# FFN up: low parts of the summed weight tiles made by an accumulating DMA in place of a VectorE subtraction

## The chip, the cores and the metric

The kernel runs on one core of a Trainium2 chip. The metric is the device time of one execution in microseconds. The time before is the median of three runs. All views come from one profiled execution; their times count from the start of its span.

## The reference, cut to what matters

The model is one block of a decoder trunk over 512 tokens of width 1024: a mixer with three branches, then a ConvGLU feed-forward network with 2816 inner columns. The change lies in the feed-forward part, in its first product, `h @ w_up`:

```python
def conv_glu_ffn(h, w_up, conv_w, w_down):
    a, g = jnp.split(h @ w_up, 2, axis=-1)
    return (jax.nn.silu(causal_dwconv(a, conv_w)) * g) @ w_down

x = x + g2 * conv_glu_ffn(h, ffn_w_up[l], ffn_conv_w[l], ffn_w_down[l])
```

Everything is float32, `w_up` is 1024 x 5632.

## The kernel before, in words

**Split operands.** TensorE works on the type fp32r. Each fp32 operand is split into a high part (ScalarE copies it into an fp32r tile, which rounds it) and a low part (the operand minus the high part). A product is three matmuls per k-tile: high by high, high by low, low by high.

**The FFN-up stage.** There are 22 column tiles m of 128 inner columns. The first two are computed plainly. For m = 2 to 21 the four blocks of one tile, two halves of the columns of `a` and `g` by two halves of the tokens, are computed with seven products in place of eight (a Strassen-Winograd scheme). Each product (`product`, L1049) has 4 k-tiles of three matmuls with 256 moving columns, so one m has 7 x 12 = 84 matmuls. Two of the operands on the weight side are raw blocks (w1, w2, tile `wa`), one is a raw block held in a free piece of another tile (w4, `up_22`, L1041), and four are sums of blocks:

- `up_s(m)` (L1028) loads the raw tile of `g` columns (SP queue, 512 KB) and builds two sum tiles `s12` and `s34` of 128 x 1024 fp32 (tag `fS`, two buffers, so each tile has one buffer that is used again for the next m). Four GpSimd instructions of 128 x 512 write them: L1034 and L1035 make `s12`, L1036 and L1037 make `s34`.
- `pair` (L1011) then splits a sum tile into `shi` (ScalarE, L1016) and `slo` (VectorE, L1017). These tiles lie in a ring `ws` of three buffers, so the next `shi` of a place waits until TensorE has finished the products that read the old one.
- `up_a(m)` (L1023) loads the raw tile of `a` columns and splits it with the same `pair`, into tiles `whi`, `wlo` (also L1016 and L1017).

The raw tiles share a ring of four buffers (`wraw`, L147). The loads of the `a` and `g` columns alternate on SP's queue; a load of `g` columns takes over the buffer of an earlier `a` tile and waits for L1037 (the last sum that reads that tile); a load of `a` columns takes over that of an earlier `g` tile and waits for the subtraction of `up_22` (L1046).

**The loop over m** (L1165 and after) has on TensorE, in this order: product 5 of m, product 1 of m+2, product 4 of m-1, product 6, product 3, product 2 of m+2, product 7. VectorE and ScalarE take partial results out of the banks between them: L1176 (ScalarE copies p5), L1185 (VectorE, p6), L1186 (GpSimd adds p1 to p5), L1194, L1195 and L1201 (VectorE, sums that end a block), the convolution `conv3` (L689 on ScalarE, L690 and L691 on VectorE), the silu (L1197) and the product with the gate (L1202). Product 7 writes over the bank that L1185 reads, product 4 over the bank that L1195 reads.

**What sets the order.** Every engine runs its queue in program order, and SP's and GpSimd's DMA issues stand in such queues too. The framework puts the instructions of each engine into an order by priorities: those under `tc.high_priority(offset=4000)` (sums and splits) come ahead of ordinary ones, those under `urgent()` (offset 9000: work on the banks) ahead of both. It also sets the semaphores for data dependencies and for buffers that are used again.

Of the kernel before, what the change touches and what calls it, by code (L numbers as in the profile page):

```python
# [15 lines left out]
AF = mybir.ActivationFunctionType  # L16
ALU = mybir.AluOpType
# [42 lines left out]
def hybrid_block(ctx, tc, ins, out, consts, dbg=None, stop=99):  # L60
    nc = tc.nc
    PE, ACT, DVE, POOL, SP = nc.tensor, nc.scalar, nc.vector, nc.gpsimd, nc.sync
# [17 lines left out]
    def T(name, shape, dt=F32, tag=None, bufs=1, pool=None):  # L80
        return (pool or sb).tile(shape, dt, name=name, tag=tag or name, bufs=bufs)
# [375 lines left out]
    for p in range(4):  # L457
# [52 lines left out]
        for w0 in range(0, 9, 4):  # L510
# [7 lines left out]
            lo = 1 if w0 == 0 else 0  # L518
# [61 lines left out]
    for rnd in range(2):  # L580
        for u0 in (0, 16):
# [11 lines left out]
            for hh in range(2):  # L593
                q = slice(hh * 64 + 32 * (1 - rnd), hh * 64 + 32 * (1 - rnd) + 32)
                src = ps[q].rearrange("p (u s) -> p u s", u=16)
# [412 lines left out]
    cut = lambda w, r: tuple(x[:, r] for x in w)  # L1008
    ws = ("s", 3)

    def pair(shape, src, ring=None):  # L1011

        pool, tag, bufs = (wp.pool, "w", 3) if ring is None else (fs.pool,) + ring
        with tc.high_priority(offset=4000):
            hi, lo = (T(tag + n, shape, F32R, bufs=bufs, pool=pool) for n in ("hi", "lo"))
            ACT.activation(hi, src, AF.Copy)  # L1016
            DVE.tensor_tensor(lo, src, hi, op=ALU.subtract)  # L1017
        return hi, lo

    up, raw_a, raw_22 = {}, {}, {}  # L1020
# [2 lines left out]
    def up_a(m):  # L1023
        raw_a[m] = up_raw(m * 128)
        wa = pair([128, 8, 128], raw_a[m])
        up[m] = {1: cut(wa, k1), 2: cut(wa, k2)}

    def up_s(m):  # L1028
        ra, rg = raw_a.pop(m), up_raw(DFF + m * 128)
        raw_22[m] = rg[:, 4:8]  # L1030
        a11, a12, a21, a22 = ra[:, 0:4], ra[:, 4:8], rg[:, 0:4], rg[:, 4:8]
        s12, s34 = (T("fS", [128, 8, 128], bufs=2, pool=fs.pool) for _ in range(2))
        with tc.high_priority(offset=4000):
            POOL.tensor_tensor(s12[:, 0:4], a21, a22, op=ALU.add)  # L1034
            POOL.tensor_tensor(s12[:, 4:8], s12[:, 0:4], a11, op=ALU.subtract)  # L1035
            POOL.tensor_tensor(s34[:, 0:4], a11, a21, op=ALU.subtract)  # L1036
            POOL.tensor_tensor(s34[:, 4:8], a12, s12[:, 4:8], op=ALU.subtract)  # L1037
        w12, w34 = pair([128, 8, 128], s12, ws), pair([128, 8, 128], s34, ws)
        up[m].update({5: cut(w12, k1), 6: cut(w12, k2), 7: cut(w34, k1), 3: cut(w34, k2)})

    def up_22(m):  # L1041
# [45 lines left out]
    def w_o(k0, hf, ring=None):  # L1087
        raw = load_raw([128, 2, 512], [((lambda r: r), dram("w_o", k0 * 128 * D + hf * 512, [[D, 128], [128 * D, 2], [1, 512]]))])
        return pair([128, 2, 512], raw, ring)
# [46 lines left out]
    for m in range(plain, plain + ahead):  # L1136
        up_a(m)
        if m == plain:
            up_s(m)
        x_first(m)  # L1140
        x_second(m)
# [23 lines left out]
    for m in range(plain, 22):  # L1165
        if m + ahead < 22:
            up_a(m + ahead)
        if m + 1 < 22:
            up_s(m + 1)
# [144 lines left out]
```

## Time and profile before

| what | value |
|---|---|
| median of 3 runs | 1208.91 us (1205.43 to 1214.12) |
| the profiled execution's own time | 1200.61 us |
| its span, first to last instruction | 1198.9 us |
| TensorE, share of the span busy | 90% |
| VectorE, share of the span busy | 69% |
| FFN-up loop in steady course | about 842 to 1055 us |

The span is 1.7 us shorter than the execution's own time. Busy shares are means over stages with different limits, so the stage that is changed has to be read by itself.

### The profile page before, as it was taken

To read this page: it belongs to the slowest core of one execution; us is meant where nothing else is said; L and a number is where in the kernel's file an instruction comes from. 1 tells how busy PE (TensorE), PEld (TensorE's weight loads), DVE (VectorE), ACT (ScalarE), POOL (GpSimd) and SP (SyncE) were. 2 spreads that over 40 slices of the span, in tenths; PEclk is the share of its full clock that TensorE was granted. 3 is DMA by queue.
4 is the path that set the end of the run, shared out by engine and by line. 5 is a ranking of instruction groups with operands and counts; after the bars stand their busy time and mean duration, and the time that the engine had idled before them with its cause. 6 is when DMAs were issued, how large, how long until landed. Compare 5 with 4: busy or idle time off the path is not lost. (4 is left out here: it accounts for less than half of the span.)

```text
span 1198.9 us, 18180 instructions
## 1 busy us (share of the span) xinstructions
PE 1074.5 (90%) x6962; PEld 876.1 (73%) x6962; DVE 824.0 (69%) x1405; ACT 463.2 (39%) x800; POOL 412.6 (34%) x289
## 2 busy tenths in 40 slices
PE   4888899799999989985898999998988888799996
PEld 3766677577667867873666678888987888788885
DVE  5888767732688739896465644489898999882326
ACT  4343422142334333321333433356554544552213
POOL 4233224322222433664444100024666666500001
PEclk9799999899999989997897999999999999999999
DMA  9642123421337981489654353522233323463201
GB/s 324 182 106 58 41 58 93 101 51 54 115 98 207 312 221 53 132 219 245 174 156 114 101 143 104 176 102 64 83 88 89 89 88 89 124 219 100 99 5 71
DMA packets 191078, 148.31 MB, mean 124 GB/s; under 512 B 18148, under 2 KB 167038, under 8 KB 190990
## 3 DMA queue, kind: packets, MB, share of 16 engines
q1 hardware_dynamic: 162605, 122.57, 35.3%
q10 hardware_dynamic: 23056, 14.53, 4.0%
q0 software_dynamic: 5328, 10.03, 3.6%
q8 instruction: 55, 0.90, 0.3%
q14 instruction: 34, 0.27, 0.1%
HBM read 128.48 MB, written 18.63 MB: 123 GB/s over the span
## 5 line engine op out<-in xcount | busy, mean ns | idle before, releaser
L165 POOL TENSOR_TENSOR wlo<-wraw,whi 128x1024 fp32r<-128x1024 f32 (+1 forms) x70 | 158.0, 2259 | 269.8 <-ACT whi L163 221.3
L177 PE MATMUL mm<-h_hi,whi 128*128 128x512 f32 (+2 forms) x496 | 200.9, 406 | 0.7 <-DVE o_cv L702 0.7
L178 PE MATMUL mm<-h_lo,whi 128*128 128x512 f32 (+2 forms) x496 | 200.2, 404 | 1.2 <-DVE h_lo L1082 1.2
L179 PE MATMUL mm<-h_hi,wlo 128*128 128x512 f32 (+2 forms) x496 | 199.6, 403 | 0.0
L163 ACT ACTIVATE whi<-wraw 128x1024 fp32r<-128x1024 f32 (+1 forms) x86 | 80.0, 934 | 211.4 <-PE mm L178 101.8
L178 PEld LDWEIGHTS mm<-h_lo,whi 128*128 128x128 f32 (+1 forms) x496 | 94.8, 191 | 23.2 <-issue 2.4
L177 PEld LDWEIGHTS mm<-h_hi,whi 128*128 128x128 f32 (+1 forms) x496 | 94.6, 191 | 22.4 <-issue 3.4
L179 PEld LDWEIGHTS mm<-h_hi,wlo 128*128 128x128 f32 (+1 forms) x496 | 94.8, 191 | 21.2 <-issue 1.4
L1017 DVE TENSOR_TENSOR wlo<-wraw,whi 128x1024 fp32r<-128x1024 f32 x39 | 50.8, 1302 | 42.2 <-ACT whi L1016 42.2
L217 DVE SCALAR_TENSOR_TENSOR acc<-xraw,ccol,acc 128x512 f32<-128x512 f32 x56 | 60.4, 1078 | 25.5 <-DMA xraw<-in_ada_w 25.0
L1053 PE MATMUL sd<-mg_hi,shi 128*128 128x256 f32 x240 | 69.3, 289 | 9.1 <-DVE p L1185 8.8
L1034 POOL TENSOR_TENSOR fS<-wraw 128x512 f32<-128x512 f32 x20 | 29.4, 1469 | 129.8 <-DVE wk L991 84.4
L1055 PE MATMUL sd<-mg_hi,slo 128*128 128x256 f32 x240 | 67.8, 283 | 0.0
L1054 PE MATMUL sd<-mg_lo,shi 128*128 128x256 f32 x240 | 67.8, 282 | 0.0
L1016 ACT ACTIVATE whi<-wraw 128x1024 fp32r<-128x1024 f32 x39 | 41.3, 1058 | 64.8 <-PE sd L1240 24.8
L1017 DVE TENSOR_TENSOR slo<-fS,shi 128x1024 fp32r<-128x1024 f32 x40 | 60.6, 1516 | 0.4 <-ACT shi L1016 0.3
L1053 PEld LDWEIGHTS sd<-mg_hi,shi 128*128 128x128 f32 x240 | 45.8, 191 | 11.4 <-DVE p L1185 11.3
L1053 PE MATMUL mm<-h_hi,whi 128*128 128x256 f32 x160 | 45.5, 285 | 3.4 <-ACT p L1066 3.0
L1281 POOL TENSOR_TENSOR f<-f 128x512 f32<-128x512 f32 x4 | 5.7, 1416 | 124.6 <-ACT wk L993 124.6
L721 DVE TENSOR_SCALAR mk<-posq,thr 128x512 f16<-128x512 f32 (+3 forms) x128 | 45.7, 430 | 3.1 <-PE sd L727 3.1
L1016 ACT ACTIVATE shi<-fS 128x1024 fp32r<-128x1024 f32 x40 | 42.1, 1052 | 12.6 <-PE sd L1054 12.6
L1054 PEld LDWEIGHTS sd<-mg_lo,shi 128*128 128x128 f32 x240 | 45.8, 191 | 0.0
(513 smaller groups left out, 2883.7 us busy)
## 6 DMA issues: line engine op xcount, KB each, us to landing
wraw<-in_w_in SPq DMA_DIRECT2D x61, 512.0 KB, 4.2
xraw<-in_ada_w SPq DMA_DIRECT2D x96, 256.0 KB, 4.3
wraw<-in_ffn_w_up SPq DMA_DIRECT2D x44, 512.0 KB, 3.9
wraw<-in_ffn_w_down SPq DMA_DIRECT2D x22, 512.0 KB, 3.5
wraw<-in_w_branch SPq DMA_DIRECT2D x24, 256.0 KB, 3.8
bias_d<-stage ACTq DMA_DIRECT2D x10, 512.0 KB, 5.3
wraw<-in_w_o SPq DMA_DIRECT2D x8, 512.0 KB, 3.9
z_att<-wk ACTq DMA_DIRECT2D x12, 256.0 KB, 2.4
```

The costliest lines, as they stand in the source:

```text
L163: ACT.activation(hi, raw, AF.Copy)
L165: lo_engine[0].tensor_tensor(lo, raw, hi, op=ALU.subtract)
L177: PE.matmul(ps, hi[:, k, :], ahi[:, k0 + k, :], start=start and k == 0, stop=False)
L178: PE.matmul(ps, hi[:, k, :], alo[:, k0 + k, :], start=False, stop=False)
L179: PE.matmul(ps, lo[:, k, :], ahi[:, k0 + k, :], start=False, stop=stop and k == kt - 1)
L217: DVE.scalar_tensor_tensor(acc, raw, ck, acc, op0=ALU.mult, op1=ALU.add)
L721: DVE.tensor_scalar(m_[:, :n], posq[:, b * 128:], thr[:, b, gg:gg + 1], None, op0=ALU.is_ge)
L1016: ACT.activation(hi, src, AF.Copy)
L1017: DVE.tensor_tensor(lo, src, hi, op=ALU.subtract)
L1053: PE.matmul(ps, at(w[0], k), b[0][:, k], start=first and k == 0, stop=False, skip_group_check=True)
L1054: PE.matmul(ps, at(w[0], k), b[1][:, k], start=False, stop=False, skip_group_check=True)
L1055: PE.matmul(ps, at(w[1], k), b[0][:, k], start=False, stop=k == 3, skip_group_check=True)
```

## The change

`pair` gets a flag `by_dma`. With it, ScalarE writes the negated high part into the low tile (a copy with scale -1), and GpSimd issues a DMA that adds the fp32 sum tile onto it: lo = -hi + src. The two calls in `up_s` set the flag; the splits of raw tiles, of `w_o`, `w_down` and of `up_22` stay as they are.

```diff
-    def pair(shape, src, ring=None):
+    def pair(shape, src, ring=None, by_dma=False):
 
         pool, tag, bufs = (wp.pool, "w", 3) if ring is None else (fs.pool,) + ring
         with tc.high_priority(offset=4000):
             hi, lo = (T(tag + n, shape, F32R, bufs=bufs, pool=pool) for n in ("hi", "lo"))
             ACT.activation(hi, src, AF.Copy)
-            DVE.tensor_tensor(lo, src, hi, op=ALU.subtract)
+            if by_dma:
+                ACT.activation(lo, hi, AF.Copy, scale=-1.0)
+                POOL.dma_start(lo, src, accum_op=ALU.add)
+            else:
+                DVE.tensor_tensor(lo, src, hi, op=ALU.subtract)
         return hi, lo
...
-        w12, w34 = pair([128, 8, 128], s12, ws), pair([128, 8, 128], s34, ws)
+        w12, w34 = pair([128, 8, 128], s12, ws, True), pair([128, 8, 128], s34, ws, True)
```

## Rows read from the trace of the kernel before

**Rows 1.** The page, part 1: busy time of an engine, share, instructions.

```profile
span 1198.9 us, 18180 instructions
...
PE 1074.5 (90%) x6962; PEld 876.1 (73%) x6962; DVE 824.0 (69%) x1405; ACT 463.2 (39%) x800; POOL 412.6 (34%) x289
```

**Rows 2.** By stretch: length, PE, PEld, DVE, ACT, POOL busy, clock, DMA share, GB/s.

```profile
865.00:925.00 60.00, 51.87 (x422) 49.82 (x420) 53.60 (x54) 28.39 (x45) 37.97 (x26) 1.00 0.31 89
925.00:975.00 50.00, 43.16 (x354) 41.93 (x355) 45.30 (x48) 23.48 (x37) 31.27 (x22) 1.00 0.31 91
```

**Rows 3.** Who waited for whom, 842 to 1055 us: total us, times, longest.

```profile
POOL fS L1036 <- DVE slo L1017: 28.9, 17, 4.7
...
PE sd L1053 <- DVE wk L1195: 19.3, 18, 3.1
```

**Rows 4.** Groups by line and form, 842 to 1055 us: busy, mean ns, idle before.

```profile
L1017 DVE TENSOR_TENSOR slo<-fS,shi 128x1024 fp32r<-128x1024 f32 x36 | 55.2, 1534 | 0.4 <-ACT shi L1016 0.3
```

**Rows 5.** Timeline of GpSimd: start us, us, instruction, idle before and its releaser.

```profile
839.77 1.55 POOL L1034 TENSOR_TENSOR fS<-wraw 128x512 f32<-128x512 f32 x1 [2.63 <-DMA wraw<-in_ffn_w_up]
...
957.74 1.34 POOL L1034 TENSOR_TENSOR fS<-wraw 128x512 f32<-128x512 f32 x1 [0.37 <-DMA wraw<-in_ffn_w_up]
...
963.19 1.77 POOL L1037 TENSOR_TENSOR fS<-wraw,fS 128x512 f32<-128x512 f32 x1
...
968.93 1.30 POOL L1034 TENSOR_TENSOR fS<-wraw 128x512 f32<-128x512 f32 x1 [1.36 <-DMA wraw<-in_ffn_w_up]
...
1027.61 1.30 POOL L1034 TENSOR_TENSOR fS<-wraw 128x512 f32<-128x512 f32 x1 [1.33 <-DMA wraw<-in_ffn_w_up]
```

**Rows 6.** Timeline of TensorE, first and last of 35 matmuls without a wait.

```profile
949.68 0.28 PE L1054 MATMUL sd<-mg_lo,shi 128*128 128x256 f32 x1
...
953.69 0.27 PE L1055 MATMUL mm<-h_hi,wlo 128*128 128x256 f32 x1
```

**Rows 7.** Tile fS, its instructions over the whole span: duration ns min/median/max.

```profile
L1016 ACT ACTIVATE shi<-fS x40: 1037/1047/1072, 803.1 to 1054.7; 128x1024 fp32r<-128x1024 f32 x40
L1017 DVE TENSOR_TENSOR slo<-fS,shi x40: 1207/1226/1981, 804.8 to 1055.8; 128x1024 fp32r<-128x1024 f32 x40
L1034 POOL TENSOR_TENSOR fS<-wraw x20: 1291/1392/1845, 780.2 to 1038.3; 128x512 f32<-128x512 f32 x20
L1036 POOL TENSOR_TENSOR fS<-wraw x20: 1288/1296/1402, 781.9 to 1045.6; 128x512 f32<-128x512 f32 x20
L1035 POOL TENSOR_TENSOR fS<-fS,wraw x20: 1291/1616/2162, 783.2 to 1039.7; 128x512 f32<-128x512 f32 x20
L1037 POOL TENSOR_TENSOR fS<-wraw,fS x20: 1287/1758/2272, 785.0 to 1046.9; 128x512 f32<-128x512 f32 x20
```

**Rows 8.** Line L978, plain 512 KB loads issued by GpSimd: issue ns, landing us.

```profile
L978 POOL DMA_DIRECT2D x<-in_x x4: 531/531/588, 684.0 to 693.9; - x4
...
DMA to landing us min/median/max: 3.9/4.4/6.0
```

**Rows 9.** Tile qi, eight DMAs of 192 KB issued by GpSimd into fp32r.

```profile
DMA to landing us min/median/max: 7.2/10.4/11.9
```

**Rows 10.** DMA queues in 683 to 699 us: packets, MB, share of 16 engines.

```profile
q0 software_dynamic: 580, 2.11, 41.2%
```

**Rows 11.** DMA in 842 to 1055 us: SP's queue, its issues with median landing.

```profile
q1 hardware_dynamic: 34283, 20.44, 32.2%
...
wraw<-in_ffn_w_up SPq DMA_DIRECT2D x32, 512.0 KB, 3.9
```

**Rows 12.** Line L147 on SP's queue, 842 to 1055 us: what its loads waited for.

```profile
SPq L147 <- POOL fS L1037: 89.1, 18, 11.0
```

**Rows 13.** Busy time by stretch where TensorE had gaps: columns as in rows 2.

```profile
542.00:544.00 2.00, 0.76 (x3) 0.48 (x3) 1.97 (x5) 0.12 (x1) 0.00 (x0) 1.00 1.42 200
544.00:546.00 2.00, 0.73 (x3) 0.59 (x3) 1.03 (x2) 0.00 (x0) 0.00 (x0) 0.82 1.22 290
546.00:548.00 2.00, 2.00 (x6) 1.12 (x6) 0.00 (x0) 0.00 (x0) 0.00 (x0) 0.50 1.20 300
```

## The prediction

> **What bounds the kernel now.** I read the page first. By its first part TensorE looks like the limit and VectorE is busy in two thirds of the span [rows 1]; that is a mean over stages, so the stage of the change has to be cut out. The table by stretch does that: in two stretches of the FFN-up loop VectorE is busy 53.60 of 60 us and 45.30 of 50 us (89% and 91%), TensorE 86%, with the clock at its upper level, 1.00 (2.4 GHz) [rows 2]. So here VectorE is close to full, and TensorE has gaps. The waits say who makes them: the first matmul of a product waits 19.3 us for L1195 on VectorE, in 18 iterations [rows 3]. The group that the change removes holds 55.2 us of VectorE in this stretch, 36 subtractions of 1.53 us [rows 4]; the other four of the 40 [rows 7] lie ahead of it.
>
> The period of one m: L1034 starts at 839.77 and, 16 iterations later, at 1027.61 (15 further starts between them) [rows 5], so (1027.61 - 839.77) / 16 = 11.74 us. TensorE alone would need less: 34 matmuls start between 949.68 and 953.69 [rows 6], 0.118 us each, times 84 = 9.9 us. VectorE's work is 0.9 x 11.74 = 10.6 us, of it 2 x 1.53 = 3.1 us for the two subtractions.
>
> So there are 1.8 us per m to win, if nothing else closes the loop first. Two other loops are nearly as long already. One is the sum buffers: each sum tile has one buffer, and L1036 waits 28.9 us in 17 iterations for the subtraction that reads the old `s34` [rows 3]. The other is the raw tiles: SP's load waits for L1037 (89.1 us in 18 cases) [rows 12], lands 3.9 us after issue [rows 11], and only then L1034 of the next m starts: L1037 ends at 963.19 + 1.77 = 964.96, L1034 starts at 968.93 [rows 5].
>
> **The change part by part.**
>
> *Removed:* 40 subtractions on VectorE. VectorE falls from 10.6 to 7.6 us per m and is no longer near the period. Its cover for this claim is TensorE's 9.9 us; what is late next is not VectorE. GpSimd's sums overlap fewer two-operand instructions and come nearer to their fastest: L1034 and L1035 have medians of 1.39 and 1.62 us, L1036 and L1037 1.30 and 1.76 us, all with a minimum of 1.29 us [rows 7]. I take 2.8 us for a pair of sums, between 2.6 and 3.1.
>
> *Added on ScalarE:* 40 copies of the form of `shi`, 1.05 us each [rows 7], 2.1 us per m. ScalarE is at 47% (28.39 of 60) [rows 2], 5.6 us per m; with 7.7 us it stays below TensorE's 9.9. As throughput it costs nothing; as latency it costs all of its 1.05 us, because the DMA waits for it.
>
> *Added on GpSimd:* 40 DMA issues, 0.53 us each by the plain load of the same size [rows 8]. GpSimd had 37.97 us busy in 60 [rows 2], 7.4 us per m; shorter sums and two issues leave it at about 7.5. But the issue waits for ScalarE, and behind it in the queue stand the sums of the next m and L1186, whose result L1195 needs before TensorE may go on. That is the new wait.
>
> *Added on the DMA engines:* 2 x 512 KB per m. The trace of before has no accumulating DMA and no copy inside SBUF, so D, the time from issue to landing, is bounded by neighbours. Below: a plain 512 KB load by the same queue, alone, 3.9 us at its fastest [rows 8]; nothing excludes that an SBUF source is a little quicker, but TensorE and the raw loop then bind, so a smaller D gains nothing. Above: the DMAs into fp32r in a crowd, 10.4 us in the median [rows 9]. My value: the median plain load, 4.4 us [rows 8]; plus one more pass, because the old destination is read too: 2.11 MB (four of these loads and a small one) held 41.2% of 16 us [rows 10], 6.6 us, so about 1.6 us each; plus 1.0 us, my allowance for meeting the raw loads, which hold 32.2% of the engines already [rows 11]. D = 4.4 + 1.6 + 1.0 = 7.0 us, an estimate.
>
> The Trainium skill has a statement on the second read: in "Collectives: The Full Stack", section "The bandwidth ceiling: the fold count and why AG ≠ RS ≠ AR", the addition in the DMA path is said to cost nothing by itself, but to need two source reads on one ring, so that it runs at half the rate. No run here shows it yet; the pass of 1.6 us agrees with it in kind, and by half a rate alone D would be 6.0 and the sum about 18 us smaller.
>
> *The new loop.* A sum buffer is free for the next m only when the DMA that reads it has landed. Around the loop: two sums 2.8, high part 1.05, negated copy 1.05, DMA D, and five hand-overs between engines, 0.4 in all (an allowance) = 5.3 + D. Both tiles have such a loop. To it I add 0.6 us for the two in-order queues (the copy behind other work on ScalarE, the issue behind a sum on GpSimd), my estimate from instructions of 0.4 to 1.4 us on queues that are 60 to 70% full. T = 5.3 + 0.6 + 7.0 = 12.9 us against 11.74: +1.16 us per m, times 18 iterations (m = 4 to 21, the first two are prepared under earlier work) = +21 us. The end and the other stages don't change.
>
> On the profiled execution: 1200.6 + 21 = 1221.6 us. That execution was quicker than the median of the three runs, 1208.9 us; the forecast is for a median, so 1208.9 + 21 = **1230 us**.
>
> The bounds of D give the range. With D = 3.9 the loop is 9.2 us, below TensorE's 9.9; then the raw loop binds: 3.97 us from L1037's end to L1034's start, four sums 5.3 us, two issues 1.06 us = 10.3 us, -1.4 x 18 = -26 us, 1183 us. With D = 10.4 it is 16.3 us, +4.6 x 18 = +82 us, 1291 us.
>
> **The rivals.**
>
> *Rival 1, the accumulate is quick and VectorE's relief counts (faster).* If the second read is hidden behind the write and the queue is not crowded, D is 3.9 to 4.7, the buffer loop 9.2 to 10.6 us, and the period 10.3 to 10.6: -20 to -26 us, about 1186 us. For it: the DMA engines were idle two thirds of the time [rows 11], and VectorE's 19.3 us of TensorE waits do go away [rows 3]. Against it: the fastest landing is that of an idle moment, and here two loads and two accumulates share each period. It decides at 5.3 + 0.6 + D = 11.74, so at D = 5.8.
>
> The Trainium skill speaks for this one: "DMA: Bandwidth & Descriptors", section "Anatomy of one DMA — SWDGE (gpsimd) path", gives about 2 us plus the bytes at 436 GB/s, which for two reads of 512 KB would be 2.0 + 2.4 = 4.4 us, an estimate from that page; the sum by it would be -24 us. The plain loads here landed in 4.4 us with one read, where that formula gives 3.2, so the trace is slower than the page.
>
> *Rival 2, one loop replaces another of the same length (no change).* D between 5.2 and 6.4: period 11.1 to 12.3, within 12 us of 1209. For it: two loops, that over VectorE and that over the sum buffers, were within a microsecond of each other before.
>
> *Rival 3, the two DMAs come to stand in a row (much slower).* The issue for `s34` of m may be queued on GpSimd behind L1034 and L1035 of the next m, which wait for the landing of the DMA for `s12`; then L1036 waits for a second whole landing. The loop becomes 2 D plus four sums 5.3 and an issue 0.5: 15 us at D = 4.5, 20 us at D = 7: +55 to +145 us, 1265 us and more. TensorE would then idle a third to a half of each period, and the trace shows what can follow gaps: with TensorE busy 0.76 and 0.73 of 2 us, the granted clock went from 1.00 to 0.82 and then 0.50, the lower level, 1.2 GHz [rows 13]; this would add more. Against it: by the priorities all of these have one rank, and a queue order that holds back a ready issue is not what they ask for.
>
> That the low part would not come from the DMA at all (the change not doing what it says) I hold for unlikely, since no subtraction is left to make it.
>
> **How the numbers follow.** Forecast 0.43 (its own range 1215 to 1255), rival 1 0.22, rival 2 0.2, rival 3 0.15. Within 1% is what a measurement of this kernel can hardly tell from no change; 1% is 12 us. Faster by more: 0.22, all of rival 1. Same: rival 2, 0.2. Slower: the forecast and rival 3, 0.58. The range goes from the lower to the upper bound of D, 1183 to 1291; it leaves out most of rival 3 and a little at the lower end.
>
> **What would show it.** Right: no subtraction of `fS` on VectorE and VectorE near 60% in the loop; L1034 and L1036 waiting for a DMA into `slo` in nearly every iteration; landing times of these DMAs between 6 and 8 us; the period from one L1034 to the next at 12 to 13.5 us; TensorE waiting for `slo`, no more for L1195. Wrong: landings under 5 us with a period near 10.4 us and TensorE waiting for nothing long (rival 1); a period that stands at 11.7 (rival 2); an issue that waits behind L1035 for another DMA's landing, and a period over 15 us with a clock below 1.00 (rival 3).

## The result, and the profile after

The changed kernel takes 1337.48 us in the median of four runs (1326.12 to 1343.41), the kernel before 1207.17 us beside it; the ratio is 1.1107, 95% interval 1.1045 to 1.117. That is 130 us slower. The forecast was 1230 us with a range up to 1291, so the direction was right and the size far off: the time lies where rival 3 put it. In some executions the granted clock is lower and the time one or two per cent longer; the ratios in this document leave those out on both sides, the medians do not.

The page of the kernel after, total and part 1, against [rows 1]:

```profile
span 1341.6 us, 18270 instructions
...
PE 1121.9 (84%) x6962; PEld 918.8 (68%) x6962; DVE 746.6 (56%) x1365; ACT 503.5 (38%) x840; POOL 425.8 (32%) x329
```

VectorE has 40 instructions and 77 us less, ScalarE 40 copies and 40 us more, GpSimd 40 issues. TensorE is busy 47 us longer with the same 6962 matmuls, and its granted clock is lower (0.80 and 0.77 in the rows below, 1.00 before). No engine got more than 40 us of new work, so most of the 130 us must be waiting. Busy time by stretch in the loop, columns as in [rows 2]:

```profile
920.00:980.00 60.00, 37.30 (x260) 36.02 (x259) 18.02 (x30) 23.11 (x33) 24.63 (x22) 0.80 0.47 106
980.00:1040.00 60.00, 37.91 (x257) 37.09 (x256) 17.61 (x25) 23.20 (x33) 25.04 (x23) 0.77 0.46 105
```

VectorE fell from 89% to 30%, TensorE from 86% to 62%, and the DMA engines are at less than half: nobody is full. Now the waits from 860 to 1190 us, which stand where [rows 3] stood:

```profile
PEld sd L1059 <- DMA slo<-fS: 119.0, 21, 9.0
PE sd L1059 <- DMA slo<-fS: 114.6, 20, 8.8
POOL fS L1038 <- DMA slo<-fS: 113.3, 16, 8.7
...
POOL fS L1040 <- DMA slo<-fS: 54.3, 14, 5.4
```

(L1038 to L1041 are the four sums L1034 to L1037 of before, L1059 is the matmul that reads the low part.) TensorE hardly waits for VectorE any more but for the new DMA, and so does GpSimd, twice per m: L1038 for one landing and L1040 for the other. The timeline of GpSimd over one period shows how the two stand to each other, and the first and last of 13 starts of L1038 give the period, as [rows 5] did:

```profile
893.26 1.27 POOL L1038 TENSOR_TENSOR fS<-wraw 128x512 f32<-128x512 f32 x1 [6.34 <-DMA slo<-fS]
...
990.86 1.27 POOL L1038 TENSOR_TENSOR fS<-wraw 128x512 f32<-128x512 f32 x1 [7.30 <-DMA slo<-fS]
992.21 1.28 POOL L1039 TENSOR_TENSOR fS<-fS,wraw 128x512 f32<-128x512 f32 x1
993.43 0.87 POOL L1019 DMA_DIRECT2D slo<-fS  x1
998.03 1.70 POOL L1040 TENSOR_TENSOR fS<-wraw 128x512 f32<-128x512 f32 x1 [3.73 <-DMA slo<-fS]
999.69 1.74 POOL L1041 TENSOR_TENSOR fS<-wraw,fS 128x512 f32<-128x512 f32 x1
1001.40 0.74 POOL L1190 TENSOR_TENSOR p<-p,p 128x256 f32<-128x256 f32 x1
1002.09 0.85 POOL L1019 DMA_DIRECT2D slo<-fS  x1
1011.63 1.27 POOL L1038 TENSOR_TENSOR fS<-wraw 128x512 f32<-128x512 f32 x1 [8.69 <-DMA slo<-fS]
...
1015.10 0.86 POOL L1019 DMA_DIRECT2D slo<-fS  x1
...
1124.58 1.27 POOL L1038 TENSOR_TENSOR fS<-wraw 128x512 f32<-128x512 f32 x1 [6.48 <-DMA slo<-fS]
```

The period is (1124.58 - 893.26) / 12 = 19.28 us against 11.74; 7.54 us more in each of the 17 steps from the third start of this sum to its last is 128 us, nearly the whole loss of 130 us. (The two profiled executions differ by more, 142.7 us, but 13 us of that lie ahead of the first sum, where nothing was changed.) Each issue is followed by a sum that waits for its landing. ScalarE's timeline over the same period says when the issues could have gone out:

```profile
993.52 1.06 ACT L1016 ACTIVATE shi<-fS 128x1024 fp32r<-128x1024 f32 x1 [3.88 <-POOL fS L1039]
...
994.75 1.05 ACT L1018 ACTIVATE slo<-shi 128x1024 fp32r<-128x1024 f32 x1
...
1001.47 1.06 ACT L1016 ACTIVATE shi<-fS 128x1024 fp32r<-128x1024 f32 x1 [3.60 <-POOL fS L1041]
1002.56 1.06 ACT L1018 ACTIVATE slo<-shi 128x1024 fp32r<-128x1024 f32 x1
```

The negated copy of `s12` (after L1039) is ready at 995.80 and its DMA is issued at 1002.09, 6.3 us later; that of `s34` (after L1041) is ready at 1003.62 and is issued at 1015.10, 11.5 us later. (This period is the longest of the twelve, 20.8 us; the medians of the two delays are 5.9 and 9.3 us.) In between GpSimd's queue holds sums that wait for the landing of the other DMA, and works them off. So the two landings lie one behind the other: 4.6 us (993.43 to 998.03), two sums and L1190, then 9.5 us here (1002.09 to 1011.63; the median is 8.2 us), two sums, and round again. Averaged over the twelve periods, the two landings take 4.81 and 8.14 us, the four sums with L1190 6.33 us: together the 19.28 us, with nothing left over.

The landings over the whole span, from the view of the tile `slo`:

```profile
DMA to landing us min/median/max: 4.5/6.5/9.8
```

### The profile page after: what moved, and what is told of

Its sections match the earlier page's. It is cut to its first block, busy times and chain, and to the rows that moved or that the text cites. A ratio compares the mean times of both kernels' runs of the same rounds, so it can differ in the third digit from the quotient of the medians.

```text
span 1341.6 us, 18270 instructions
## 1 busy us (share of the span) xinstructions
PE 1121.9 (84%) x6962; PEld 918.8 (68%) x6962; DVE 746.6 (56%) x1365; ACT 503.5 (38%) x840; POOL 425.8 (32%) x329
## 5 line engine op out<-in xcount | busy, mean ns | idle before, releaser
L1059 PE MATMUL sd<-mg_hi,slo 128*128 128x256 f32 x240 | 79.9, 333 | 116.3 <-DMA slo<-fS 116.3
L1059 PEld LDWEIGHTS sd<-mg_hi,slo 128*128 128x128 f32 x240 | 54.4, 227 | 120.0 <-DMA slo<-fS 120.0
L1038 POOL TENSOR_TENSOR fS<-wraw 128x512 f32<-128x512 f32 x20 | 25.5, 1273 | 213.7 <-DMA slo<-fS 118.1
L1016 ACT ACTIVATE whi<-wraw 128x1024 fp32r<-128x1024 f32 x39 | 41.3, 1058 | 122.4 <-DMA wraw<-in_ffn_w_up 73.0
L1058 PE MATMUL sd<-mg_lo,shi 128*128 128x256 f32 x240 | 74.7, 311 | 1.6 <-DVE mg_lo L1086 1.6
L1057 PE MATMUL sd<-mg_hi,shi 128*128 128x256 f32 x240 | 75.0, 313 | 0.7 <-ACT mg_hi L1085 0.5
L1205 DVE TENSOR_TENSOR wk<-sd,p 128x256 f32<-128x256 f32 x20 | 8.5, 424 | 84.6 <-PE sd L1059 84.6
L1058 PEld LDWEIGHTS sd<-mg_lo,shi 128*128 128x128 f32 x240 | 52.7, 220 | 1.8 <-DVE mg_lo L1086 1.8
L1057 PEld LDWEIGHTS sd<-mg_hi,shi 128*128 128x128 f32 x240 | 52.8, 220 | 1.7 <-DVE p L1189 1.0
L1057 PE MATMUL mm<-h_hi,whi 128*128 128x256 f32 x160 | 53.0, 331 | 1.0 <-ACT p L1070 1.0
L1058 PE MATMUL mm<-h_lo,whi 128*128 128x256 f32 x160 | 52.4, 328 | 0.0
```

The source lines that it names most:

```text
L1057: PE.matmul(ps, at(w[0], k), b[0][:, k], start=first and k == 0, stop=False, skip_group_check=True)
L1058: PE.matmul(ps, at(w[0], k), b[1][:, k], start=False, stop=False, skip_group_check=True)
L1059: PE.matmul(ps, at(w[1], k), b[0][:, k], start=False, stop=k == 3, skip_group_check=True)
```

## The experiments

Theory: the order of GpSimd's queue puts two landings in a row into the loop (rival 3), and what is left is the loop of the single sum buffer. Rivals: the accumulating transfers are simply too slow or too many for the DMA engines; ScalarE's copies are part of the loss. The kernel before was run anew beside each group of runs (medians of 1202.70 to 1208.00 us); ratios are to that.

**e1_order.** The next sums are placed behind both issues (`issued[0]` is the DMA issue made last, and `issue_after` puts what follows behind it in the queue):

```diff
-                POOL.dma_start(lo, src, accum_op=ALU.add)
+                issued[0] = POOL.dma_start(lo, src, accum_op=ALU.add).ins
...
-        with tc.high_priority(offset=4000):
+        with tc.high_priority(offset=4000), tc.issue_after(issued[0]) if issued[0] else nullcontext():
             POOL.tensor_tensor(s12[:, 0:4], a21, a22, op=ALU.add)
```

> Edit: the four sums of the next m are placed behind both DMA issues of this m in GpSimd's queue; nothing else changes. Queue theory (a sum that waits for one landing stands ahead of the other DMA's ready issue, so the two landings lie one behind the other in the loop): the landings now overlap, the period of one m falls from 19.3 us to one landing of 6 to 8 us, four sums 5.2, high part and negated copy 2.1, one issue 0.9, about 14.5 to 16 us; the whole 60 to 90 us below the changed kernel, 1250 to 1280 us. DMA theory (the transfers themselves are too slow, in whatever order): the two transfers crowd each other, landings go to 10 us and more, and the period stays near 19 us, 1320 to 1345 us.

Measured: 1246.49 us, ratio to before 1.0366 (1.0287 to 1.0446), a little quicker than the theory had it. L1041, the first sum here, starts 14 times between 895.32 and 1077.70: a period of 14.0 us. GpSimd's timeline, and the landings from the view of the tile `slo`:

```profile
895.32 1.28 POOL L1041 TENSOR_TENSOR fS<-wraw 128x512 f32<-128x512 f32 x1 [3.00 <-DMA slo<-fS]
...
988.06 0.87 POOL L1021 DMA_DIRECT2D slo<-fS  x1
989.70 0.86 POOL L1021 DMA_DIRECT2D slo<-fS  x1 [0.77 <-ACT slo L1020]
994.26 1.28 POOL L1041 TENSOR_TENSOR fS<-wraw 128x512 f32<-128x512 f32 x1 [3.71 <-DMA slo<-fS]
995.62 1.29 POOL L1042 TENSOR_TENSOR fS<-fS,wraw 128x512 f32<-128x512 f32 x1
998.20 1.29 POOL L1043 TENSOR_TENSOR fS<-wraw 128x512 f32<-128x512 f32 x1 [1.28 <-DMA slo<-fS]
...
1077.70 1.27 POOL L1041 TENSOR_TENSOR fS<-wraw 128x512 f32<-128x512 f32 x1 [3.37 <-DMA slo<-fS]
```

```profile
DMA to landing us min/median/max: 4.5/7.6/10.9
```

The same instructions, the same bytes, and landings that are longer than in the changed kernel, as the two now run side by side (its median is 7.6 us against 6.5), and yet two thirds of the loss are gone. So the order made most of the loss, not the speed of the transfers. What is left is one landing: 8.5 us from the second issue (989.70) to L1043 (998.20; 7.6 to 9.0 us over the periods, 8.2 in the mean), and 14.0 - 8.2 = 5.8 us for two sums, two copies, hand-overs and a short wait of ScalarE's copy for TensorE (5.9 us in eight cases from 900 to 1050 us).

**e10_order_plain.** e1_order with a plain copy, so that the landing alone is shorter. The low part is then the sum tile, not the difference.

```diff
-                issued[0] = POOL.dma_start(lo, src, accum_op=ALU.add).ins
+                issued[0] = POOL.dma_start(lo, src).ins
```

> Edit: e1_order (issues ahead of the next sums) with a plain copy in place of the accumulate (the low part is not the difference). The landing of the second issue falls by about 1.6 us from 8.5. One-landing loop theory (period = landing of the second DMA + 5.3 to 5.6): the period falls by the same amount, from 14.0 to about 12.4 us, 1215 to 1228 us. If e1_order is held by something other than the landing (the raw loads, ScalarE's queue), it stays at 13.5 us or more, 1240 us or more.

Measured: 1223.29 us, ratio 1.0162 (1.0095 to 1.023); 15 starts between 872.43 and 1048.91, a period of 12.6 us:

```profile
872.43 1.27 POOL L1041 TENSOR_TENSOR fS<-wraw 128x512 f32<-128x512 f32 x1 [3.53 <-DMA slo<-fS]
...
1048.91 1.27 POOL L1041 TENSOR_TENSOR fS<-wraw 128x512 f32<-128x512 f32 x1 [2.57 <-DMA slo<-fS]
```

```profile
DMA to landing us min/median/max: 2.9/5.4/7.8
```

The landing median goes from 7.6 to 5.4 us. From the second issue to L1043 it is 6.2 us in the mean against 8.2, and the period follows, by 1.4 of these 2.0 us; the rest of the loop grew, as L1043 takes 2.2 us here against 1.3. That fits the loop of one landing; neither the raw loads nor ScalarE's queue alone held e1_order at 14.0 us.

**e3_plain.** The changed kernel with the plain copy, order as in the changed kernel; again the low part is not the difference.

```diff
-                POOL.dma_start(lo, src, accum_op=ALU.add)
+                POOL.dma_start(lo, src)
```

> Edit: the same DMA without the addition (a copy of the sum tile into the low tile, so the low part is not the difference); issue order and bytes written are the same, the old destination is not read. If the addition is what makes the landing long, landings fall from 4.6 and 8.2 us to under 3.5 and the period to under 14 us (1250 us or less). If it is the order with the fixed part of a DMA and the crowd with the raw loads, landings fall by 0.5 to 1.6 us each and the period by twice that, to 16 to 18 us, 1285 to 1320 us.

Measured: 1283.32 us, ratio 1.065 (1.0568 to 1.0732), at the lower edge of the second expectation. The period is 17.0 us (14 starts from 893.53 to 1114.49) in the profiled execution, which at 1294.81 us was the longest of the four. Issue and landing, view of the tile `slo`:

```profile
L1019 POOL DMA_DIRECT2D slo<-fS x40: 568/568/585, 813.9 to 1147.7; - x40
...
DMA to landing us min/median/max: 2.9/4.3/7.9
```

Even a transfer without the addition loses 6.5% in this order, where it loses 1.6% in the order of e1 (e10_order_plain). But the length counts too: 54 of the 130 us go with the addition. The price of the addition itself is seen here: the fastest landing is 4.5 us with it and 2.9 us without, the issue 0.86 us against 0.57. The queues say the same in engine time. First the changed kernel from 900 to 1140 us (25 issues), then this one from 900 to 1080 us (21 issues):

```profile
q0 software_dynamic: 3459, 12.59, 27.4%
```

```profile
q0 software_dynamic: 3024, 11.02, 17.2%
```

27.4% of 240 us is 65.8 us for 12.59 MB, or 2.7 us for a tile of 0.524 MB; 17.2% of 180 us is 31.0 us for 11.02 MB, 1.5 us a tile. The ratio is 1.9.

**e4_only12.** Only the first sum tile by DMA:

```diff
-        w12, w34 = pair([128, 8, 128], s12, ws, True), pair([128, 8, 128], s34, ws, True)
+        w12, w34 = pair([128, 8, 128], s12, ws, True), pair([128, 8, 128], s34, ws)
```

> Edit: only the first sum tile goes by DMA, the second by the VectorE subtraction as before the change. Queue theory: one landing is left in the loop; a landing of 5 to 8 us, four sums 5.2, the p5 addition 0.7, an issue 0.9: 12 to 14.5 us, 1210 to 1255 us. DMA theory (time follows the bytes): half of the loss, about 1270 us.

Measured: 1247.24 us, ratio 1.0356 (1.0255 to 1.0457), period 13.6 us (13 starts from 893.44 to 1056.20):

```profile
893.44 1.28 POOL L1038 TENSOR_TENSOR fS<-wraw 128x512 f32<-128x512 f32 x1 [5.76 <-DMA slo<-fS]
...
1056.20 1.26 POOL L1038 TENSOR_TENSOR fS<-wraw 128x512 f32<-128x512 f32 x1 [6.08 <-DMA slo<-fS]
```

One landing in the loop costs what one landing costs in e1_order, although half the bytes are moved. The time goes by landings in a row more than by bytes: half of the loss would have been 1270 us.

**e5_dveadd.** The copies alone: ScalarE negates, VectorE adds.

```diff
-                POOL.dma_start(lo, src, accum_op=ALU.add)
+                DVE.tensor_tensor(lo, lo, src, op=ALU.add)
```

> Edit: the negated copy on ScalarE stays, but VectorE adds the sum tile onto it in place of the DMA. The two copies of 1.05 us per m are all that is new against the kernel before. If they cost only latency in a loop with slack, as the forecast took it, the period stays at 11.7 to 12.2 us and the time within 1% of before, 1200 to 1220 us. If ScalarE's in-order queue is part of the loss (rival), the period goes to 12.8 us and more, 1225 us or more.

Measured: 1202.45 us, ratio 0.9953 (0.9906 to 1.0). The 40 added copies cost nothing that can be measured as work of ScalarE. Their latency still stands in the loop of the DMA, 1.05 us of the 5.8 us in e1_order.

**e9_free.** No DMA and nothing in its place, so the sum is never added to the negated copy:

```diff
-                POOL.dma_start(lo, src, accum_op=ALU.add)
```

> Edit: the DMA is left out and nothing takes its place (the low tile keeps the negated high part, so the sum is never added): what the change would give with a transfer of no length. If VectorE's fill closed the loop of before by itself, the period falls to TensorE's 9.9 us, -33 us, about 1175 us. If the raw-tile loop stands close behind, as the forecast's lower bound took it, 10.3 to 11 us, -13 to -26 us, 1182 to 1195 us. If nothing is won (1% or less), the two other loops were as long as VectorE's.

Measured: 1195.96 us, ratio 0.9881 (0.9819 to 0.9944). This is the most that the idea could have given: 1.2% (0.6 to 1.8%), some 14 us. Busy time by stretch in its loop:

```profile
860.00:920.00 60.00, 54.79 (x449) 52.96 (x448) 39.95 (x48) 38.44 (x57) 34.47 (x27) 1.00 0.34 100
920.00:980.00 60.00, 58.83 (x489) 57.56 (x488) 42.25 (x53) 45.05 (x66) 36.66 (x26) 1.00 0.35 102
```

TensorE reaches 98% in one stretch and 91% in the other, and the period over 14 starts (854.63 to 1001.50) is 11.3 us in the profiled execution, the shortest of the ten (1180.09 us). GpSimd's sums still wait for the raw loads there, 41.3 us in 10 cases from 842 to 1040 us. So the raw-tile loop and TensorE itself, which is nearly full, are what is left; no run separates the two.

**e7_wa and e11_wa_sum.** The accumulating DMA where no sum buffer hangs on it: the raw tile of `a` columns from m = 4 on, sum tiles on VectorE as before. In e11_wa_sum the last of the four sums also moves to VectorE.

```diff
-        wa = pair([128, 8, 128], raw_a[m])
+        wa = pair([128, 8, 128], raw_a[m], None, m >= 4)
...
-            POOL.tensor_tensor(s34[:, 4:8], a12, s12[:, 4:8], op=ALU.subtract)
+            DVE.tensor_tensor(s34[:, 4:8], a12, s12[:, 4:8], op=ALU.subtract)
```

(The second edit is in e11_wa_sum alone.)

> Edit: the sum tiles are subtracted on VectorE as before; the raw tile of a columns, needed one m later and not written again soon, gets its low part by the accumulating DMA (m from 4 on). Queue theory: no sum buffer hangs on this landing, so only the issue (0.9 us on GpSimd) and the wait for ScalarE's copy are on GpSimd's queue; VectorE loses 1.4 us per m; period 11.0 to 12.2 us, 1190 to 1220 us. DMA theory (any accumulate here costs its landing): period up by several us, 1250 us or more.

> Edit: e7_wa (the raw tile of a columns by accumulating DMA, sum tiles subtracted on VectorE), and the last of the four sums moves from GpSimd to VectorE, into the time that was freed there. If the raw-tile loop and GpSimd's queue held e7_wa, the period falls by up to 1 us, -10 to -18 us against before, about 1195 us. If VectorE's in-order queue holds it, the added instruction costs its 0.7 to 1.2 us in that loop: 1220 to 1240 us.

Measured: e7_wa 1219.39 us, ratio 1.008 (1.0023 to 1.0137); e11_wa_sum 1213.96 us, ratio 1.0093 (1.0052 to 1.0133). In e7_wa the landings take 4.9 us in the median and TensorE waits for them only 7.0 us in six cases. So the same DMA, 18 times, once per m, costs under 1% where its landing is not in the loop of the sum buffers. But there is no gain either, though VectorE is at 76%:

```profile
865.00:925.00 60.00, 51.73 (x399) 50.11 (x399) 45.80 (x49) 30.23 (x46) 37.66 (x29) 0.94 0.54 125
```

e11_wa_sum missed its expectation: it is as slow as e7_wa by interval and lies between the two values that were expected, so it shows neither the one nor the other. Which wait decides there stays open.

**e2_bufs4, e8_order_bufs4 and their control e6_before_bufs4.** Two buffers for each sum tile, so that no sum would wait for the landing just before it; e6 is the kernel before (VectorE subtractions) with the same buffers, e8 has also the order of e1 (`fx[0]` is a pool opened in memory that is free by then).

```diff
-        s12, s34 = (T("fS", [128, 8, 128], bufs=2, pool=fs.pool) for _ in range(2))
+        s12, s34 = (T("fS", [128, 8, 128], bufs=2, pool=fx[0].pool if m % 2 else fs.pool) for _ in range(2))
...
-    sn = lambda name: T(name, [128, N2], bufs=2 if name != "p1" else 4, pool=fs.pool)
+    sn = lambda name: T(name, [128, N2], bufs={"p1": 4, "p6": 1}.get(name, 2), pool=fs.pool)
```

> Edit: two buffers for each sum tile in place of one (the second pair lies in memory that is free by then, p6 gets one buffer less); both pairs still by DMA. Queue theory: no sum waits for the landing of the DMA just before it, so the two-landing loop is gone; the period falls to the raw-tile loop (a load of 4.5 us, four sums 5.2, issues 1.7) of about 11 to 12.5 us, 1185 to 1225 us. DMA theory: two accumulates of 512 KB in each period still set it, 17 us or more, 1300 us or more.

> Edit: the kernel before (VectorE subtractions), with two buffers for each sum tile and one less for p6. If the loop of before was closed by VectorE's fill alone (91%), the period stays near 11.5 us, 0 to -6 us. If the wait of the sums for the old tile (28.9 us in 17 iterations) was on the path, it falls to 10.7 to 11.2 us, -10 to -18 us, about 1190 us.

> Edit: both pairs by DMA, issues ahead of the next sums as in e1_order, and two buffers for each sum tile. Queue theory with the buffer loop: e1_order was left with one landing of 8.5 us plus 5.3 us of sums and copies in the loop of the single buffer; here no sum waits for a landing. The raw-tile loop is left (load of 5 to 7 us beside the accumulates, four sums 5.2): 11 to 13 us, 1195 to 1235 us. If the bytes on the DMA engines set what e1_order was left with, nothing changes: 14 us, 1240 to 1255 us.

Measured: e2 1267.65 us, ratio 1.0525 (1.0448 to 1.0602); e6 1253.74 us, ratio 1.0372 (1.0309 to 1.0435); e8 1251.4 us, ratio 1.0299 (1.0217 to 1.0381). e2 and e6 miss whatever was expected of them; e8 falls where its rival (the bytes on the DMA engines) put it, 1240 to 1255 us. But the control says why none of this can be used: the buffers by themselves, with no such DMA, made the kernel before 3.7% slower, to the same time as e8. They changed what was held to be fixed: with them the framework orders the engines anew (in e6 and e8 GpSimd takes the first sum of `s34` ahead of the second of `s12`, in e2 an issue comes to stand between the sums). In e6 from 900 to 1050 us TensorE waits longer for VectorE's L1201 (L1195 of before) than it did in [rows 3], in fewer iterations:

```profile
PE sd L1058 <- DVE wk L1201: 35.2, 11, 5.5
```

So these runs don't prove the loop of the single buffer; whether p6's one buffer or the new order costs the 45 us stays open. It fits that loop that against e6, with the same buffers, the DMAs cost 1.5% in e2 and nothing in e8, where with one buffer they cost 11.1%, and that e2's 1267.65 us are far under the 1300 us of the DMA theory; but the order moved too. e1_order and e10_order_plain carry the point. No version tried that does the whole computation is clearly faster than the kernel before: the nearest is e5_dveadd, whose interval reaches 1.0.

## Why the prediction was right or wrong, point by point

- **What bounds the loop: right in kind, too generous in size.** VectorE was close to full, and two other loops stood close behind. e9_free, with VectorE relieved and no transfer at all, won 1.2%. The forecast's lower end and rival 1 (-20 to -26 us) took the raw loop at 10.3 us; the profiled period was 11.3, with TensorE 91 to 98% busy. Two small slips in the forecast's sums change nothing: the lower bound's loop of 9.2 us leaves out the 0.6 us of the queues, and with D = 4.4 its own loop gives -26 us, not -24.
- **The copies on ScalarE: right.** No cost as throughput (e5_dveadd, 0.9953).
- **The length of a landing: near.** The estimate was 7.0 us; the median is 6.5, but as two kinds, about 4.6 and 8.2 us. That the estimate came near is in part luck: without raw loads it had 6.0 us (4.4 + 1.6) where 4.6 was measured, and for meeting them it had 1.0 us where the later of the two DMAs has 3.6 more (8.2 against 4.6), so two errors nearly cancel. The second read was put at 1.6 us, and the fastest landings differ by just that (4.5 and 2.9). The statement of the Trainium skill that was drawn on, in "Collectives: The Full Stack", section "The bandwidth ceiling: the fold count and why AG ≠ RS ≠ AR", that the addition halves the rate because it needs a second source read, is made there of ReduceScatter beside AllGather. The 2.7 and 1.5 us of engine time per tile agree with it.
- **The loop over the sum buffer, 5.3 + 0.6 + D: right where it stands alone.** e1_order has 14.0 us, of them 8.2 from the second issue to L1043 and 5.8 from there to the next second issue. In the order that the forecast had in mind the kernel is thus slower, by 3.7%, so the direction is not luck; the other 91 us of the loss are the order.
- **The step that failed: "To it I add 0.6 us for the two in-order queues".** The wait at GpSimd's queue was taken for the chance meeting of an issue and a running sum. It is no such thing: the queue holds an instruction that waits for a landing, and everything behind it waits as long. The two issues went out 5.9 and 9.3 us after their data were ready, in the median (6.3 and 11.5 in the period shown), in place of 0.6. With that the loop has both landings: 4.81 + 8.14 + 6.33 us of sums and L1190 = 19.28 us, the measured period, against the forecast 12.9.
- **Rival 3 had the mechanism and the price** (the issue of `s34` queued behind the next L1034 and L1035; 15 to 20 us, +55 to +145 us) and was given 0.15. The argument against it, that instructions of one rank would not be ordered so as to hold back a ready issue, was wrong: the order is fixed when the program is built, before any landing is known, and the trace shows the ready issue of 1003.62 standing behind L1038 until that had its landing at 1011.63 and its two sums were done.
- **"This would add more", of the clock: not seen.** TensorE's clock does fall (below), but no wait of the loop is for TensorE: the copies wait for L1039 and L1041, those for landings. 7.54 us per period, all of it in landings and sums, makes up the loss already. (In e1_order, by contrast, ScalarE's copies do wait for TensorE, 5.9 us in eight cases.) That the clock costs nothing here is argued from the chain of waits; no run held the clock apart.

## What to carry to other kernels

Moving work from a full engine to a DMA puts a landing of several microseconds where an instruction of 1.5 us stood; before counting the engine time that is saved, draw the loop that the landing closes (the buffer that it holds, the next writer of that buffer) and read in which order the issuing queue takes the issue and that writer. Two landings that depend on each other through one in-order queue add up, even if the buffers would let them run side by side. And try first what the relief is worth with the replacement left out: here 1.2%.

## What the runs showed of the hardware

**An accumulating DMA of 512 KB inside SBUF into fp32r** takes 0.86 us to issue on GpSimd (plain 0.57), lands after 4.5 us at its fastest (plain 2.9) and holds the DMA engines 2.7 us (plain 1.5).

**Beside other loads it is far longer.** In the changed kernel the DMA that goes out right after SP's raw loads takes about 8.2 us, the other, with no raw load under way, 4.6 us. The packet records of the trace say where the difference lies. The DMA issued at 993.43 has its first packet at 994.87, 1.4 us later, and its last ends at 997.63. That issued at 982.71 has its first packet only at 987.09, 4.4 us later, when the raw loads (983.12 to 987.96) are nearly through, and its last ends at 990.45. Most of the difference is time before its first packet, not slower packets. No run moved the raw loads away.

**The clock falls during the wait.** Busy time by stretch in the changed kernel, columns as in [rows 2]:

```profile
1002.00:1004.00 2.00, 1.19 (x11) 0.98 (x9) 0.00 (x0) 1.97 (x3) 0.94 (x2) 1.00 0.55 145
...
1006.00:1008.00 2.00, 0.00 (x0) 0.00 (x0) 0.14 (x1) 0.00 (x0) 0.00 (x0) 0.54 1.09 261
1008.00:1010.00 2.00, 0.00 (x0) 0.00 (x0) 0.00 (x0) 0.00 (x0) 0.00 (x0) 0.50 0.69 136
1010.00:1012.00 2.00, 0.46 (x2) 0.46 (x3) 0.00 (x0) 0.30 (x1) 0.37 (x1) 0.50 0.04 8
1012.00:1014.00 2.00, 2.00 (x11) 2.00 (x11) 1.21 (x1) 1.03 (x2) 1.92 (x2) 0.50 0.00 0
...
1016.00:1018.00 2.00, 2.00 (x17) 2.00 (x17) 0.02 (x1) 2.00 (x5) 0.00 (x0) 0.90 0.86 164
```

The DMA engines have next to nothing to do from 1010 us on (0.04), but by the packet records the last packet of this DMA ends at 1011.16 only, and the sum that waits for it starts at 1011.63, 0.5 us later. (For the DMA issued at 993.43 it is 0.4 us, from 997.63 to 998.03.) TensorE stands still from about 1003 to 1011.5 us; the granted clock goes from 1.00 (2.4 GHz) to 0.50 (1.2 GHz), and it is still 0.50 in the stretch from 1012 to 1014 us, in which TensorE is busy throughout, and back at 0.90 from 1016 us.
